# Expert stage of a mixture-of-experts network: 64 slots for each expert in place of 128 for each group, two experts at a time in the column halves of TensorE, fp32 weights used as loaded

## The chip, the core and the metric

One core of a Trainium2 chip runs the whole network in one launch. The metric is the device time of an execution in microseconds (us); the time before is the median of three runs. Engines are named as in the profile: PE is TensorE's matmul, PEld its weight load, DVE VectorE, ACT ScalarE, POOL GpSimd, SP SyncE, whose queue issues the weight loads.

## What is computed

Two blocks with 256 tokens of width 1024. The first has two layers; each has a mixer, a residual and layer norm, and then 16 experts in four groups. The experts are what the change is about:

```python
def hier_moe(x, w_group, b_group, w_router, b_router, w_gate, w_up, w_down):
    ...
    probs_g = jax.nn.softmax((xf @ w_group + b_group).astype(jnp.float32), axis=-1)
    p_top, g_idx = lax.top_k(probs_g, 1)
    logits_e = (xf @ w_router + b_router).astype(jnp.float32).reshape(T, N_GROUPS, EXPERTS_PER_GROUP)
    in_group = jnp.take_along_axis(logits_e, g_idx[:, :, None], axis=1)[:, 0]
    probs_in = jax.nn.softmax(in_group, axis=-1)
    w_top, e_local = lax.top_k(probs_in, TOP_K_IN_GROUP)
    ...
    h = jax.nn.silu(jnp.einsum('td,edf->tef', xf, w_gate)) * jnp.einsum('td,edf->tef', xf, w_up)
    y = jnp.einsum('tef,efd->td', h * gates[:, :, None].astype(h.dtype), w_down)
```

A token goes to one group and to two of its four experts. Each expert has `w_gate` and `w_up` of 1024x256 and `w_down` of 256x1024, fp32: three times 1.05 MB, 50 MB in a layer. The second block (feed-forward parts of width 2816, a latent attention with spatial gating, a short convolution) is not touched.

## The kernel before

Products with large weights are made from two fp32r parts of each operand: `split` and `split_weights` (L130, L177) write the rounded high part on ACT and the rest on DVE, in four pieces of 512 columns, and `mm3` (L118) adds high x high, high x low and low x high.

`moe` (L790) first transposes the mixer's output and multiplies it with the router's weights, normalizes it (`xh`) and splits it (`xs`). `best` (L827) picks the group with five small DVE operations. The token's rank in its group comes from products with a triangular matrix (`pr`, L842), and `pos` is its slot. Then all engines read the largest group count and pass a branch, `tc.If(count > CAP)` (L911), whose body (`every_expert`) handles tokens beyond 128 slots; in the profiled execution it isn't entered. `slots` (L922) makes a 0/1 matrix of two groups, and `gather` (L929) multiplies the tokens with it, so that each group's tokens lie in 128 columns; the result is split again (`xg`, a ring of three groups). The second pair of groups is gathered at step 4.

The loop at L1038 goes over 16 experts. At step n PE does `turned(n-1)` (two transposes of the hidden values, split into `hT`), `up(n)` (L955: 2 x 8 x 3 matmuls of 256 columns into the bank `gu`), and `down(n-1)` (L1016: 2 x 2 x 3 matmuls of 512 columns into the two banks `yd`, which sum over a group's four experts). After each group `scatter` (L1022) splits `yd` and takes it back to token order with eight matmuls into `macc`. `gates` (L858), which needs the second-best expert too, follows the first `up`. `alpha` (L823) adds the residual by fp32 matmuls.

Every expert's load goes into a `raw` tile by SP in program order and waits for a free tile (`weight_tile`, L149); within `moe` there are two more `raw` tiles and one more of each part. In the first layer the projections of the memory for the next mixer (`memory_kv`, `keys` and `values`, L461) are passed in as filler for PE: `keys` ahead of the branch, `values` behind the first gather. Their matmuls stand in the trace partly ahead of where the program has them: the layer that orders the work puts what is ready ahead of what waits. What follows the stage: `after_moe` (L1126), then `stick` (L671), whose first loads are from `w_kv_shared` and `b_w_in`, or `ffn` (L1158).

Two places that are not changed are of use in reading the change: `even_mixer`, lines 1383 to 1393, writes two products into the two halves of the output's partitions (`ps[64 * i:64 * i + 64]`), each with 64 columns of fp32 weights, for four pairs of heads, 256 columns of moving data and then 128; and `alpha` above.

Of the kernel before, what the change touches and what calls it, by code (L numbers as in the profile page):

```python
# [11 lines left out]
F32 = mybir.dt.float32  # L12
F32R = mybir.dt.float32r
# [12 lines left out]
CAP = 128  # L26
SPLITS = 4
MOE_MORE = (2, 1)
LATER = 0
RAW0 = 0  # L30
MOE_SPARE = (6, 0, 2, 99)
# [47 lines left out]
class Net:  # L79
# [57 lines left out]
    @contextmanager  # L137
    def more_buffers(self, raw, parts, turn=0, shift=0):

        names = ("raw", "whi", "wlo")  # L140
        with self.tc.tile_pool(name="more", bufs=1) as p:
            if shift:
                self.shift(p, shift)
            self.extra = [p, dict(zip(names, (raw, parts, parts))), dict.fromkeys(names, 0)]
            self.turn = {"raw": RAW0, "whi": turn, "wlo": turn}
            yield
            self.extra = None

    def weight_tile(self, name, dt):  # L149
        pool, tag, n = self.w, name, 2  # L150
        if self.extra is not None:
            p, more, spare = self.extra
            i = self.turn[name] % (2 + more[name] + spare[name])
            self.turn[name] += 1
            if i >= 2 + more[name]:
                return self.wide_tile(name, dt)
            elif i >= 2:
                pool, n = p, more[name]
# [631 lines left out]
    def moe(self, layer, xh, filler=()):  # L790


        nc, d = self.nc, self.d
        wr, gb, const, gt, bt = self.routed
        with ExitStack() as st:
            p = st.enter_context(self.tc.tile_pool(name="moe", bufs=1))
            st.enter_context(self.more_buffers(*MOE_MORE, turn=2, shift=160))
            early = [self.expert_weights(layer, 0, "w_gate", KD)]
# [39 lines left out]

            gm, go = best(L[:, :, 0:4], "grp")
            gob = p.tile([P, 2, 4], BF, name="grp_b")  # L840
            nc.vector.tensor_copy(gob, go)
            pr = self.aux()  # L842
            self.mm(pr[:, 0:4], self.before, gob[:, 0], True, True)
            self.mm(pr[:, 4:8], self.before, gob[:, 1], True, False)
            self.mm(pr[:, 4:8], self.onesb, gob[:, 0], False, True)
            self.mm(pr[:, 8:12], self.onesb, gob[:, 0], True, False)
            self.mm(pr[:, 8:12], self.onesb, gob[:, 1], False, True)
            most = p.tile([P, 1], F32, name="most")
            nc.vector.tensor_reduce(most, pr[:, 8:12], AX.X, ALU.max)
            mosti = p.tile([P, 1], I32, name="mosti")  # L850
            nc.vector.tensor_copy(mosti, most)
            pos = p.tile([P, 2, 4], F32, name="pos")
            self.ts(pos, go, -4096.0, 4096.0, ALU.mult, ALU.add)
            self.tt(pos, pos, pr[:, 0:8].rearrange("p (a g) -> p a g", a=2), ALU.add)
            rank = p.tile([P, 8], F32, name="rank")
            nc.vector.tensor_copy(rank, pr[:, 0:8])

            def gates():  # L858

                e4 = p.tile([P, 2, 4], F32, name="g_e")  # L860
                self.tt(e4, L[:, :, 0:4], gm[:, :, None].to_broadcast([P, 2, 4]), ALU.subtract)
                self.act(e4, e4, AF.Exp)
                top = p.tile([P, 2], F32, name="p_top")
                nc.vector.tensor_reduce(top, e4, AX.X, ALU.add)
                nc.vector.reciprocal(top, top)
                sel = p.tile([P, 2, 4, 4], F32, name="sel")
                ing = p.tile([P, 2, 4], F32, name="ing")
                for tt in range(2):
                    self.tt(sel[:, tt], L[:, tt, 4:20].rearrange("p (g j) -> p g j", g=4),
                            go[:, tt, :, None].to_broadcast([P, 4, 4]), ALU.mult)  # L870
                    nc.vector.tensor_reduce(ing[:, tt], sel[:, tt].rearrange("p g j -> p j g"), AX.X, ALU.add)
                m1, o1 = best(ing, "one")
                rest = p.tile([P, 2, 4], F32, name="rest")
                self.stt(rest, o1, NEG, ing, ALU.mult, ALU.add)
                m2, o2 = best(rest, "two")
                e2 = p.tile([P, 2], F32, name="e2")
                self.tt(e2, m2, m1, ALU.subtract)
                self.act(e2, e2, AF.Exp)
                w1 = p.tile([P, 2], F32, name="w1")
                self.ts(w1, e2, 1.0, None, ALU.add)  # L880
                nc.vector.reciprocal(w1, w1)
                self.tt(w1, w1, top, ALU.mult)
                self.tt(e2, e2, w1, ALU.mult)
                gj = p.tile([P, 2, 4], F32, name="gj")
                t4 = p.tile([P, 2, 4], F32, name="t4")
                self.tt(gj, o1, w1[:, :, None].to_broadcast([P, 2, 4]), ALU.mult)
                self.tt(t4, o2, e2[:, :, None].to_broadcast([P, 2, 4]), ALU.mult)
                self.tt(gj, gj, t4, ALU.add)
                return gj

            def gates_beyond():

                gj = gates()
                t4 = p.tile([P, 2, 4], F32, name="t4")
                self.ts(t4, rank[:, 0:8].rearrange("p (a g) -> p a g", a=2), float(CAP), None, ALU.is_ge)
                self.tt(t4, t4, go, ALU.mult)
# [10 lines left out]
            for f in filler[:1]:  # L907
                f()
# [604 lines left out]
```

## Time and profile before

| | us |
|---|---|
| median of 3 runs (range) | 1634.55 (1633.69 to 1635.58) |
| the profiled execution's own time | 1639.96 |
| its span, first to last instruction | 1638.2 |
| PE busy, of the span | 1558.1 (95%) |
| DVE busy | 1189.6 (73%) |
| ACT busy | 955.6 (58%) |

Busy time of PE counts a pipelined matmul from its start to its modelled end; the distance between two starts is what a matmul costs in a row of them. In a timeline, a row is "start us, duration us, engine, line, operation, out<-in, shape, count", and several equal instructions in a row are merged; behind it in brackets stands the idle time before it and what ended it. `128*64 128x256` is a weight tile of 128 rows and 64 columns and moving data of 128x256.

### The profile page before, as it was taken

What the parts mean: (1) busy time and instruction counts of PE and PEld (TensorE: products, weight loads), DVE (VectorE), ACT (ScalarE), POOL (GpSimd) and SP (SyncE); (2) the same over time, 40 slices, a digit from 0 to 9 for tenths busy, and PEclk for the clock granted to TensorE, in tenths of its full rate; (3) what the DMA queues carried; (4) which work ended last, traced back from release to release, by engine and by line L of the source; (5) the groups of instructions that cost most, each with busy time, mean ns of one, the idle gap of its engine ahead of it and who ended that gap; (6) DMA issues with size and microseconds to landing.
All of it is one profiled execution on the core that took longest, in us unless ns stands there. A gap on an engine that the chain in (4) does not pass through costs nothing.

```text
span 1638.2 us, 27858 instructions
## 1 busy us (share of the span) xinstructions
PE 1558.1 (95%) x10908; PEld 1431.6 (87%) x10908; DVE 1189.6 (73%) x2448; ACT 955.6 (58%) x1929; POOL 37.6 (2%) x52
## 2 busy tenths in 40 slices
PE   7999879998896999989999999999999999999998
PEld 6998778997775889879988879998899989999986
DVE  6987788987566999896655787665566647766754
ACT  5566677875755887765444656544554445454533
POOL 3000100001000000010000000000000000000000
PEclk9999989999998999999999999999999999999999
DMA  7234547992435589666553547555565547555551
GB/s 230 89 122 155 196 172 275 365 333 88 137 134 198 217 309 346 251 208 206 190 183 99 178 148 226 192 194 180 185 203 186 188 141 233 204 175 193 195 176 60
DMA packets 183710, 317.72 MB, mean 194 GB/s; under 512 B 5755, under 2 KB 135728, under 8 KB 171280
## 3 DMA queue, kind: packets, MB, share of 16 engines
q1 hardware_dynamic: 180976, 309.52, 55.2%
q0 software_dynamic: 2304, 5.78, 1.2%
q8 instruction: 90, 1.47, 0.4%
q14 instruction: 52, 0.43, 0.1%
q10 hardware_dynamic: 288, 0.52, 0.1%
HBM read 314.75 MB, written 1.05 MB: 193 GB/s over the span
## 4 chain that ended last, share of the span: by engine, by line
PE 63%; DVE 2%; ACT 1%; DMA 0%; issue 0%; ACTq 0%
PE acc L116 52%; PE gu L116 5%; PE yd L116 3%; PE aux L116 2%; DVE wlo L105 1%; PE macc L116 1%; PE aux L325 1%; ACT whi L97 1%; DMA raw<-in_w_up_dram 0%; ACT xTh L97 0%; PE gu L1006 0%; PE aux L1374 0%; ACT xgh L97 0%; DVE nt_u L113 0%; DVE ln_st L420 0%
## 5 line engine op out<-in xcount | busy, mean ns | idle before, releaser
L97 ACT ACTIVATE whi<-raw 128x512 fp32r<-128x512 f32 (+3 forms) x1204 | 653.0, 612 | 475.4 <-issue 239.8
L105 DVE TENSOR_TENSOR wlo<-raw,whi 128x512 fp32r<-128x512 f32 (+3 forms) x1204 | 758.5, 677 | 192.2 <-ACT whi L97 190.0
L116 PE MATMUL acc<-xTh,wlo 128*128 128x256 f32 x1824 | 507.4, 278 | 4.3 <-DVE wlo L105 4.3
L116 PE MATMUL acc<-xTh,whi 128*128 128x256 f32 x1824 | 508.3, 279 | 1.2 <-ACT xTh L97 1.2
L116 PE MATMUL acc<-xTl,whi 128*128 128x256 f32 x1824 | 507.7, 279 | 1.2 <-DVE xTl L105 1.1
L116 PEld LDWEIGHTS acc<-xTh,wlo 128*128 128x128 f32 x1824 | 344.4, 189 | 5.6 <-DVE wlo L105 5.1
L116 PEld LDWEIGHTS acc<-xTl,whi 128*128 128x128 f32 x1824 | 344.6, 189 | 2.5 <-DVE xTl L105 1.7
L116 PEld LDWEIGHTS acc<-xTh,whi 128*128 128x128 f32 x1824 | 344.3, 189 | 2.2 <-ACT xTh L97 1.8
L116 PE MATMUL gu<-whi,xgh 128*128 128x256 f32 x512 | 147.8, 289 | 0.0
L116 PE MATMUL gu<-whi,xgl 128*128 128x256 f32 x512 | 144.9, 283 | 2.1 <-DVE xgl L105 2.1
L116 PE MATMUL gu<-wlo,xgh 128*128 128x256 f32 x512 | 145.0, 283 | 0.8 <-DVE wlo L105 0.8
L116 PE MATMUL acc<-whi,hTl 128*128 128x512 f32 x352 | 137.7, 391 | 0.0
L116 PE MATMUL acc<-wlo,hTh 128*128 128x512 f32 x352 | 137.7, 391 | 0.0
L116 PE MATMUL acc<-whi,hTh 128*128 128x512 f32 x352 | 137.7, 391 | 0.0
L116 PEld LDWEIGHTS gu<-whi,xgl 128*128 128x128 f32 x512 | 97.7, 191 | 3.4 <-DVE xgl L105 3.3
L116 PEld LDWEIGHTS gu<-wlo,xgh 128*128 128x128 f32 x512 | 97.6, 191 | 1.7 <-DVE wlo L105 1.2
L116 PEld LDWEIGHTS gu<-whi,xgh 128*128 128x128 f32 x512 | 97.8, 191 | 0.6 <-DVE hTl L105 0.2
L105 DVE TENSOR_TENSOR u<-acc,rms_R 128x512 f32<-128x512 f32 x44 | 30.4, 691 | 84.0 <-PE acc L116 83.8
L116 PEld LDWEIGHTS acc<-whi,hTl 128*128 128x128 f32 x352 | 66.1, 188 | 14.5
L116 PEld LDWEIGHTS acc<-wlo,hTh 128*128 128x128 f32 x352 | 66.1, 188 | 14.4
L116 PEld LDWEIGHTS acc<-whi,hTh 128*128 128x128 f32 x352 | 66.1, 188 | 14.4
L105 DVE TENSOR_TENSOR g<-acc,rms_R 128x512 f32<-128x512 f32 x44 | 30.4, 691 | 40.6 <-PE acc L116 40.6
(428 smaller groups left out, 2146.9 us busy)
## 6 DMA issues: line engine op xcount, KB each, us to landing
raw<-in_w_gate_dram SPq DMA_DIRECT2D x32, 1024.0 KB, 5.1
raw<-in_w_up_dram SPq DMA_DIRECT2D x32, 1024.0 KB, 5.3
raw<-in_w_down_dram SPq DMA_DIRECT2D x32, 1024.0 KB, 5.3
raw<-in_ffn_pre_w_gate_dram SPq DMA_DIRECT2D x22, 1024.0 KB, 5.4
raw<-in_ffn_pre_w_up_dram SPq DMA_DIRECT2D x22, 1024.0 KB, 5.4
raw<-in_ffn_post_w_gate_dram SPq DMA_DIRECT2D x22, 1024.0 KB, 5.2
raw<-in_ffn_post_w_up_dram SPq DMA_DIRECT2D x22, 1024.0 KB, 5.3
raw<-in_ffn_pre_w_down_dram SPq DMA_DIRECT2D x20, 1024.0 KB, 5.0
```

The costliest lines, as they stand in the source:

```text
L97: return self.nc.scalar.activation(out, in_, func, **kw)
L105: return self.nc.vector.tensor_tensor(out, a, b, op=op)
L116: self.last_mm = self.nc.tensor.matmul(out, lhsT, rhs, start=start, stop=stop, skip_group_check=True)
L325: self.nc.tensor.transpose(pv[:, i, tt * P:(tt + 1) * P], src(k + i, tt), self.ident)
```

## The change

- Each expert has 64 slots of its own (`CAP`), so a layer has 16 x 64 slots in place of 4 x 128; `best` is run for both experts ahead of the ranking, and the rank is counted per expert.
- Gathered tokens (`xg`) and hidden values (`hT`) are kept in fp32, unsplit; weights are used from the tile into which they were loaded.
- `up(n)` and `down(n)` handle experts 2n and 2n+1: one writes partitions 0 to 63 of the bank and the other 64 to 127, each with 64 columns of stationary data. The loop has eight pairs. `yd` is no longer summed over a group, and each pair is scattered, one step later (`behind`).
- Loads go into ten tiles in turn (`EXPERT_ROOM`): four new ones and the two each of `raw`, `whi` and `wlo`. The first ten are asked for at the head of `moe`, six more behind each `up`.
- `w_down` is read with rows p and 128 + p on a partition in place of 2p and 2p + 1.
- The branch stands behind `gather(0)`, both `slots` and the gates; `keys` and `values` both stand ahead of `gather(0)`. The second gather is at step 1, `alpha` at steps 5 and 6.
- `every_expert` has other tiles and loads `w_down` separately. `more_buffers` loses options that only `moe` used.

```diff
-CAP = 128
+CAP = 64
-MOE_MORE = (2, 1)
+EXPERT_ROOM = ("more", "more", "more", "more", "raw", "raw", "whi", "wlo", "whi", "wlo")
...
-            early = [self.expert_weights(layer, 0, "w_gate", KD)]
+            self.more = st.enter_context(self.tc.tile_pool(name="more", bufs=1))
+            self.asked = 0
+            wanted = [(name, 2 * n + i) for n in range(8) for name in ("w_gate", "w_up", "w_down") for i in range(2)]
+            loaded = {}
+
+            def fetch(n):
+                for name, ex in wanted[:n]:
+                    loaded[name, ex] = self.expert_weights(layer, ex, name)
+                del wanted[:n]
+
+            fetch(len(EXPERT_ROOM))
...
+            for tt in range(2):
+                self.tt(sel[:, tt], L[:, tt, 4:20].rearrange("p (g j) -> p g j", g=4),
+                        go[:, tt, :, None].to_broadcast([P, 4, 4]), ALU.mult)
+                nc.vector.tensor_reduce(ing[:, tt], sel[:, tt].rearrange("p g j -> p j g"), AX.X, ALU.add)
+            m1, o1 = best(ing, "one")
+            rest = p.tile([P, 2, 4], F32, name="rest")
+            self.stt(rest, o1, NEG, ing, ALU.mult, ALU.add)
+            m2, o2 = best(rest, "two")
+            both = p.tile([P, 2, 4], F32, name="both")
+            self.tt(both, o1, o2, ALU.add)
+            M = p.tile([P, 2, 4, 4], F32, name="members")
+            for tt in range(2):
+                self.tt(M[:, tt], both[:, tt, None, :].to_broadcast([P, 4, 4]),
+                        go[:, tt, :, None].to_broadcast([P, 4, 4]), ALU.mult)
...
+            S = self.wide_tile("S", F32R).rearrange("p (a e c) -> p a e c", a=2, e=16)
+
+            def slots(half):
+                es = slice(8 * half, 8 * half + 8)
                 for tt in range(2):
+                    self.tt(S[:, tt, es], self.slots[:, None, 0:CAP].to_broadcast([P, 8, CAP]),
+                            pos[:, tt, es, None].to_broadcast([P, 8, CAP]), ALU.is_equal)
+
+            xg = [p.tile([P, KD, 8 * CAP], F32, name=f"xg{i}") for i in range(2)]
+
+            def gather(half):
+                Sf = S[:, :, 8 * half:8 * half + 8].rearrange("p a e c -> p a (e c)")
+                for k in range(KD):
+                    pv = self.aux()
+                    for tt in range(2):
+                        for part in range(2):
+                            self.mm(pv, xs[part][:, tt, k], Sf[:, tt], tt + part == 0, tt + part == 2)
+                    g, b = gb[:, 0, k:k + 1], gb[:, 1, k:k + 1]
+                    if k % 2:
+                        self.act(xg[half][:, k], pv, AF.Identity, scale=g, bias=b)
+                    else:
+                        self.ts(xg[half][:, k], pv, g, b, ALU.mult, ALU.add)
+
+            for f in filler:
+                f()
+            slots(0)
+            gather(0)
+            slots(1)
...
             count = nc.values_load(mosti[0:1, 0:1], min_val=0, max_val=T)
             with self.tc.If(count > CAP):
...
+            def up(n):
                 ps = self.aux("gu")
+                for part, name in enumerate(("w_gate", "w_up")):
+                    w = [loaded[name, 2 * n + i].rearrange("p (k f) -> p k f", k=KD) for i in range(2)]
                     for k in range(KD):
+                        for i in range(2):
+                            o = (2 * (n % 4) + i) * CAP
+                            self.mm(ps[64 * i:64 * i + 64, part * 256:(part + 1) * 256],
+                                    xg[n // 4][:, k, o:o + CAP], w[i][:, k], part + k == 0, k == KD - 1)
                 return ps
...
+            def slot_gates():
+                pg = self.aux()[:, 0:8 * 48].rearrange("p (n c e) -> p n c e", n=8, c=3)
+                for n in range(8):
+                    for tt in range(2):
+                        self.mm(pg[:, n], Sb[tt][:, n * P:(n + 1) * P], g3[:, tt], n + tt == 0, tt == 1)
+                for i in range(2):
+                    for n in range(8):
+                        rows = slice(64 * i, 64 * i + 64)
+                        nc.vector.tensor_reduce(gs[rows, n:n + 1], pg[rows, n, :, 2 * n + i], AX.X, ALU.add)
...
+            def turned(n, ps, h):
+
+                for k in range(2):
+                    nc.tensor.transpose(ps[:, k * P:(k + 1) * P], h[:, k * P:(k + 1) * P], self.ident)
                 for tt in range(2):
+                    nc.tensor.transpose(ps[:, (2 + tt) * P:(3 + tt) * P],
+                                        S[:, tt, 2 * n:2 * n + 2].rearrange("p e c -> p (e c)").bitcast(F32), self.ident)
...
+            def down(n, hT, yd):
+                w = [loaded["w_down", 2 * n + i].rearrange("p (k f) -> p k f", k=2) for i in range(2)]
                 for half in range(2):
                     for k in range(2):
+                        for i in range(2):
+                            self.mm(yd[half][64 * i:64 * i + 64], hT[:, k, 64 * i:64 * i + 64],
+                                    w[i][:, k, half * 512:(half + 1) * 512], k == 0, k == 1)
...
+            for n in range(9):
                 if ahead is not None:
+                    m, ps0, h0, done = ahead
+                    hT, ST = turned(m, ps0, h0)
+                if n < 8:
+                    ps = up(n)
+                    if n == 0:
+                        with self.tc.issue_after(parted.ins):
+                            for tt in range(2):
+                                self.act(Sb[tt], S[:, tt].rearrange("p e c -> p (e c)").bitcast(F32), AF.Copy)
+                        slot_gates()
+                    now = (n, ps) + gated(n, ps)
+                    fetch(6)
+                if behind is not None:
+                    scatter(*behind)
+                    behind = None
                 if ahead is not None:
+                    yd = [self.aux("yd") for _ in range(2)]
+                    down(m, hT, yd)
+                    behind = m, ST, parts(yd)
+                if n == 1:
+                    gather(1)
...
+            scatter(*behind)
...
-        return self.weights(self.d[name][layer, ex].rearrange("(p k) f -> p k f", k=k), k, 2048 // k)
...
+        room = EXPERT_ROOM[self.asked % len(EXPERT_ROOM)]
+        self.asked += 1
...
+        if room == "more":
+            to = self.more.tile([P, 2048], F32, name="more", bufs=4)
+        else:
+            size = 2048 if room == "raw" else 2080
+            to = self.w.tile([P, size], F32, name="e" + room, tag=room, bufs=2)[:, 0:2048]
+        self.nc.sync.dma_start(to.rearrange("p (k f) -> p k f", k=src.shape[1]), src)
+        return to
```

## Rows read from the trace of the kernel before

**Rows 1.** The page: busy us, share of the span, and instructions of each engine.
```profile
PE 1558.1 (95%) x10908; PEld 1431.6 (87%) x10908; DVE 1189.6 (73%) x2448; ACT 955.6 (58%) x1929; POOL 37.6 (2%) x52
```

**Rows 2.** Instructions of `gu` and `macc`, each layer: ns min/median/max, first and last start.
```profile
L116 PE MATMUL gu<-whi,xgh x256: 276/281/682, 210.3 to 374.1; 128*128 128x256 f32 x128
L116 PE MATMUL gu<-whi,xgh x256: 276/281/682, 536.4 to 687.2; 128*128 128x256 f32 x128
L116 PE MATMUL macc<-yl,ST x8: 387/396/398, 349.2 to 383.0; 128*128 128x512 f32 x8
L116 PE MATMUL macc<-yl,ST x8: 387/397/475, 662.7 to 696.1; 128*128 128x512 f32 x8
```

**Rows 3.** Windows: length; PE, PEld, DVE, ACT, POOL busy; clock, DMA share, GB/s.
```profile
210.00:383.00 173.00, 160.93 (x1083) 145.97 (x1083) 150.54 (x296) 132.22 (x261) 1.62 (x3) 0.96 0.75 278
536.00:698.00 162.00, 157.04 (x1085) 142.36 (x1083) 148.00 (x284) 127.30 (x254) 0.53 (x1) 1.00 0.77 288
600.00:620.00 20.00, 20.00 (x139) 18.04 (x139) 19.96 (x36) 16.92 (x34) 0.00 (x0) 1.00 1.01 397
```

**Rows 4.** Timeline of PE: neighbours in `down` and in the first `up`.
```profile
300.06 0.39 PE L116 MATMUL yd<-whi,hTl 128*128 128x512 f32 x1
300.29 0.39 PE L116 MATMUL yd<-whi,hTh 128*128 128x512 f32 x1
...
536.36 0.28 PE L116 MATMUL gu<-whi,xgh 128*128 128x256 f32 x1
536.48 0.28 PE L116 MATMUL gu<-wlo,xgh 128*128 128x256 f32 x1
```

**Rows 5.** Groups by line over the span: busy us, mean ns, idle before.
```profile
L105 DVE TENSOR_TENSOR wlo<-raw,whi 128x512 fp32r<-128x512 f32 (+3 forms) x1204 | 758.5, 677 | 192.2 <-ACT whi L97 190.0 <-ACT scx L97 0.4
L97 ACT ACTIVATE whi<-raw 128x512 fp32r<-128x512 f32 (+3 forms) x1204 | 653.0, 612 | 475.4 <-issue 239.8 <-PE acc L116 180.6 <-DMA raw<-in_a_w_in_dram 13.8
L116 PE MATMUL macc<-x,alpha 128*128 128x512 f32 x16 | 7.8, 592 | 0.0
```

**Rows 6.** Timeline of PE: one fp32 product, products in column halves, the one behind.
```profile
273.25 1.02 PE L116 MATMUL macc<-x,alpha 128*128 128x512 f32 x2
...
974.83 2.82 PE L116 MATMUL aux<-pT,vs 128*64 128x256 f32 x32
977.58 0.50 PE L116 MATMUL acc<-whi,mixTh 128*128 128x512 f32 x1
```

**Rows 7.** DMA issues from 492 to 698 us: count, KB each, median us to landing.
```profile
raw<-in_w_gate_dram SPq DMA_DIRECT2D x15, 1024.0 KB, 5.2
```

**Rows 8.** Timeline of SP's queue: first layer's end, second layer's start.
```profile
364.13 0.38 SPq L170 DMA_DIRECT2D raw<-in_w_kv_shared_dram  x1
...
491.62 0.34 SPq L170 DMA_DIRECT2D raw<-in_w_gate_dram  x1
...
517.43 0.33 SPq L170 DMA_DIRECT2D raw<-in_w_up_dram  x1
544.40 0.34 SPq L170 DMA_DIRECT2D raw<-in_w_down_dram  x1
```

**Rows 9.** Window, instructions of `wlo` alone: length; PE, PEld, DVE busy; clock, DMA.
```profile
503.00:517.00 14.00, 4.63 (x12) 2.07 (x11) 7.84 (x13) 1.00 0.58 195
```

**Rows 10.** Timeline of the second layer's routing: selection, and behind the branch.
```profile
521.49 0.16 DVE L830 TENSOR_REDUCE grp_m<-logits 128x2 f32<-128x8 f32 x1
521.68 0.17 DVE L105 TENSOR_TENSOR grp_o<-logits,grp_m 128x8 f32<-128x8 f32 x1
...
529.92 0.87 DVE L109 TENSOR_SCALAR S<-c,pos 128x128 fp32r<-128x128 f32 x4 [4.51 <-DVEq L911]
530.55 0.55 PE L116 MATMUL aux<-S,xsh 128*128 128x256 f32 x1 [5.60 <-DVE S L109]
```

**Rows 11.** Timeline of PE: neighbours in the first gather of the second layer.
```profile
530.90 0.41 PE L116 MATMUL aux<-S,xsl 128*128 128x256 f32 x1
531.11 0.41 PE L116 MATMUL aux<-S,xsh 128*128 128x256 f32 x1
```

**Rows 12.** Windows, all engines: columns as in Rows 3.
```profile
220.00:240.00 20.00, 14.44 (x93) 13.62 (x93) 12.83 (x35) 12.63 (x24) 0.00 (x0) 0.74 0.49 181
500.00:520.00 20.00, 16.97 (x97) 14.41 (x95) 17.76 (x46) 14.77 (x23) 0.00 (x0) 1.00 0.67 231
```

More of the change, by code (lines that the diff above doesn't have):

```diff
@@ L839, in moe @@
             gm, go = best(L[:, :, 0:4], "grp")
[L840 to L847 removed]
+            sel = p.tile([P, 2, 4, 4], F32, name="sel")
@@ L854, in moe @@
[L854 to L867, printed above, removed]
-                for tt in range(2):
[L869 to L889, printed above, removed]
@@ L949, in moe @@
-            Ss = {0: slots(0)}
-            gather(0, Ss[0])
-            early.append(self.expert_weights(layer, 0, "w_up", KD))
-            for f in filler[1:]:
-                f()
-            def up(g, ws):
+                over = p.tile([P, 2, 16], F32, name="over")
+                self.ts(over, pos, float(CAP), None, ALU.is_ge)
+                self.tt(over, over, G, ALU.mult)
+                self.every_expert(p, layer, x, xh, gb, xf, over)
+                nc.scalar.preload_act_table_set("silu_and_others")
@@ L1024, in scatter, with parts @@
+            def parts(yd):
+                out = []
                 for half in range(2):
@@ L1026, in scatter @@
                     yl = p.tile([P, 512], F32R, name="yl", bufs=2)
-                    scattered = self.split(yh, yl, yd[half])
-                    parts.append((yh, yl))
+                    self.scattered = self.split(yh, yl, yd[half])
+                    out.append((yh, yl))
+                return out
+            def scatter(n, ST, y):
                 for half in range(2):
@@ L1031, in scatter @@
                         for i in range(2):
-                            self.mm(acc[tt][half], ST[:, tt * P:(tt + 1) * P], parts[half][i],
-                                    g + i == 0, g + i == 4)
-                return scattered
+                            self.mm(acc[tt][half], ST[:, tt * P:(tt + 1) * P], y[half][i], n + i == 0, n + i == 8)
             acc = [[self.bank("macc") for _ in range(2)] for _ in range(2)]
-            ahead, slot = None, {}
-            for n in range(17):
-                g, e = divmod(n, 4)
-                if n == MOE_SPARE[0]:
-                    self.extra[2].update(raw=MOE_SPARE[1], whi=MOE_SPARE[2], wlo=MOE_SPARE[2])
-                if n == MOE_SPARE[3]:
-                    self.extra[2].update(raw=0, whi=0, wlo=0)
-                if ahead is not None:
-                    g0, e0, ps0, h0, last, done = ahead
-                    hT = turned(ps0, h0)
-                if n < 16:
-                    ps = up(g, self.gate_and_up(layer, n)) if n else first
-                    if e:
-                        now = (g, e, ps) + gated(slot[g][0], e, ps)
-                if ahead is not None:
-                    if e0 == 0:
-                        yd = [self.aux("yd") for _ in range(2)]
-                    down(e0, hT, self.expert_weights(layer, n - 1, "w_down", 2), yd)
-                    if e0 == 3:
-                        scattered = scatter(g0, yd, slot[g0][1])
-                if n < 16 and e == 0:
-                    slot[g] = by_slot(g)
-                    now = (g, e, ps) + gated(slot[g][0], e, ps)
```

213 lines of the change are left out of this document (83 added, 130 removed).

## The prediction, made before the changed kernel ran

> **What bounds the kernel now.** The first view is the page's busy line: PE has 95% of the span, DVE 73%, ACT 58% [rows 1]; the reader should take from it only that no engine is idle on average and that the stage has to be looked at by itself. The change touches only the two expert stages. They run from the first matmul into `gu` (210.3 and 536.4 us) to the last scatter (383.0 and 696.1 us, 0.4 us long) [rows 2]: 173 and 160 us. The windows over them show PE busy for 161 and 157 us at a granted clock of 0.96 and 1.00, DVE for 151 and 148 us, and DMA at 0.75 to 0.77 of its time [rows 3]. So four resources lie close together, and what the change is worth depends on the second one, not on PE's saving alone.
>
> One expert now costs PE 48 matmuls of 256 columns that start 0.12 us apart, 12 of 512 columns 0.23 us apart, two transposes and a quarter of eight scatter matmuls [rows 4]: 48 x 0.12 + 12 x 0.23 + 0.24 + 0.46 = 9.2 us. The splits cost DVE 12 x 0.68 = 8.1 us, ACT 12 x 0.61 = 7.3 us per expert [rows 5]. Its three loads of 1.049 MB take 3 x 2.64 = 7.9 us at the 397 GB/s that the window 600 to 620 holds with DMA at 1.01 [rows 3]. PE binds, DVE and DMA are 12 to 14% behind. 16 x 9.2 = 147 us of each stage is this; the other 13 to 26 us are the second gather, the `alpha` products and waits.
>
> **Part 1: PE's work per pair of experts.** The new matmuls take fp32 operands. The row of `macc<-x,alpha` counts 16 instructions for the 8 products in the code, so one fp32 product is two passes [rows 5]; the two passes of one 512-column product take 1.02 us together with 0.59 us for the second, so one pass starts 0.43 us after the other [rows 5, 6]. That is 0.84 ns a column and pass: 0.43 us for an fp32 product of 256 columns, 0.86 us for 512. Two products into the two halves of the columns: lines 1383 to 1393 make 8 of 256 and 8 of 128 columns this way, 32 instructions in 2.82 us with the tail of the last [rows 6]. In a row they would take 8 x 0.43 + 8 x 0.215 = 5.2 us; without the tail of about 0.27 us it is half of that. The halves do run beside each other. A pair of experts then costs PE: gate and up 16 steps x 0.43 = 6.9 us, down 4 x 0.86 = 3.4, four transposes at most 0.5, eight scatter matmuls 8 x 0.23 = 1.8: 12.6 us, against 18.4 now.
>
> The Trainium skill speaks against this in "TensorEngine Tiling (Array Packing)", section Key Properties: a change of tiling mode drains the engine. The trace shows such a change as a duration of 0.50 us for the first full matmul behind the halves [rows 6], against 0.39 us [rows 4]; at four changes a pair by that price it would be 0.4 us, which lies in waits that the next part finds.
>
> **Part 2: loads.** A pair needs six loads: 6 x 2.64 = 15.9 us, above PE's 12.6. So the stage goes over from PE to the loads. They are issued by SP in order, into ten buffers, the first ten ahead of the router, and each later one waits until its buffer's last reader is done. A load of its own takes 5.2 us from issue to landing [rows 7]. The ten are asked for at about 491 us (the first load now goes at 491.6 [rows 8]) and need some 30 us; the first product comes at about 540 us, so they are there. SP now issues nothing between 517.4 and 544.4 us in this stretch [rows 8]; that pause stays, since all ten buffers are full.
>
> In the steady part two things compete. By bandwidth a pair takes 15.9 us. By the ring: the up weights of pair n+2 go into the buffers that down(n) frees, and down(n) stands behind up(n+1) on PE: half of up 3.4 + scatter 1.8 + down 3.4 + 5.2 to landing + 2.6 for the second = 16.4 us. I take 16.5.
>
> **Part 3: splits removed.** All 48 x 4 splits per stage on ACT and DVE go: 192 x 0.68 = 130 us of DVE and 192 x 0.61 = 117 us of ACT [rows 5], hidden behind PE today. Worth nothing in the steady part. In the routing stretch they stand between the small operations on DVE: 7.8 us of `wlo` between 503 and 517 us [rows 9]. I take 4 us of gain in the second layer and 2 in the first, where part of them belongs to the memory projection and stays. Ends: 0 and 7.8.
>
> **Part 4: routing and gather.** Eighteen small DVE operations move ahead of the ranking (selection of two experts, membership): they start 0.2 us apart [rows 10], 3.6 us on the path. Slots: two operations of 128x512 at 0.68 us [rows 5] ahead of the gather in place of two or four of 0.2 to 0.3: +0.5. gather(0) has 32 matmuls of 512 columns where 256 stood: at the full clock 32 x 0.23 = 7.4 us, at the clock that PE has after its idle time 0.21 us per 256 columns [rows 11], so 13.7; I take 10.5, the middle. Now 32 of them take 5.8 us (530.55 to 536.36) [rows 10, 4]: +4.7 us in the second layer; in the first, twenty `values()` matmuls that now stand among them move ahead, so +1.7. The branch moves behind the gather: PE's 5.6 us and DVE's 4.5 us of idle time there [rows 10] are paid once in either place. Bounds: 0, if the gather's evictions cover it, to +5 if PE is cold once more behind it. The POOL issues that wait at the branch feed only the stage's end. First product: 536.4 + 3.6 + 0.5 + 4.7 - 4 = 541 us; first layer 210.3 + 3.6 + 0.5 + 1.7 - 2 = 214 us.
>
> The branch is not taken: routing the inputs by the reference gives at most 40 tokens for an expert in the first layer and 44 in the second, under 64.
>
> **Part 5: the stage from its first product.** up(0) 6.9 us, 3 more for the low clock; loads restart when the gate half is used, at 6 us. up(2)'s weights are there 5.2 + 5 x 2.64 later, at 24 us, if down(0) is early; if PE does slot gates, up(1) and down(0) strictly in order and waits some 3.5 us for the sixteen small reductions before the first transposes, down(0) ends at 25 and they land at 33. Five more pairs at 16.5: 107 or 116. Behind the last up weights: 3.4 + scatter 1.8 + down(6) 3.4 + 0.5 + scatter 1.8 + down(7) 3.4 + eviction of two halves 2.2 + scatter 1.8 = 18 us. 125 or 134; I take 129, and 3 us for dips of the clock (below): 132. gather(1), 7.4 us, the `alpha` products, 3.4, and slot gates lie in the 4 us that PE waits in each pair. ACT and DVE lose more than they gain.
>
> What follows: kv_shared went at 364.1 us, 19 us ahead of the end [rows 8]; behind the change it waits in SP's queue for a buffer that up(7) frees, some 15 us ahead of the end, and 5.2 us suffice. Cost nothing; without that cover up to 5 us.
>
> **Sum.** First layer: 214 + 132 = 346 against 383.4: -37. Second: 541 + 132 = 673 against 696.5: -23.5. The profiled execution took 1639.96 us (span 1638.2); less 60.5 it is 1579.5. The median of the runs lies 5.4 us lower, so 1574 us.
>
> **Rivals.** (a) PE's clock falls in every pair, because PE now waits for loads. For it: between 220 and 240 us, where PE was busy 14.4 of 20 us with waits between, the granted clock averaged 0.74, so 2.4 GHz and 1.2 GHz by turns; 12.6 of 16.5 us is not far from that. Against it: 17.0 of 20 us kept 1.00 between 500 and 520 [rows 12]. The waits here would be two of 2 to 3 us per pair. At 0.74 PE's pair is 17 us and the ring 8.6 / 0.74 + 7.8 = 19.4, three more than I took, over seven pairs and a longer tail about 25 us per layer: 60 - 50, 1624 us. The Trainium skill states it as a rule in "TensorE: Matmul & The Clock Gate", section HAM oscillation: short bursts with load waits between them go back to half clock each time. By that rule the trace's 0.74 is the case to expect; 1.00 at 17 of 20 us is where the trace does not bear it out.
>
> (b) Slower than before: the halves don't overlap in this form, since here both halves read fresh weights at every step where the case of rows 6 did so for 16 products. Then gate and up take 13.8 us, down 6.9, a pair 23; PE binds, 8 x 23 + 7.4 + 3.4 + 18 = 213 us from the first product: +44 and +58 against now, 1634 + 102 = 1736. It decides from a pair time of about 18 us on. Rows 6 are against it. A milder form on the same side is (a) with the clock at 1.2 GHz through the stage, 25 us per pair, but a PE that is busy without a pause got 1.00 in this trace.
>
> (c) The ring does not bind and the loads come at full rate: no splits, down early, first product as early as now. 120 us from 212 and 537: -51 and -39, 1544 us. For it: work that is ready was put ahead in this kernel (the `values()` matmuls among the gather's). Against: it needs every one of these.
>
> (d) The change doesn't do what it says: an expert overflows and the fallback runs, 48 more loads a layer at 5.2 us, 250 us each. Only other inputs would do that.
>
> **Chances.** Forecast 0.62; (a) 0.18; (c) 0.10; (b) and its milder form 0.08; (d) and others 0.02. Bounds: the unknown prices of parts 3 to 5 move a layer by -12 to +14 us, two layers 1550 to 1602; (c) adds 1544 below, and half of (a) up to 1612 above. Range 1542 to 1612. A measurement of this kernel tells 0.2%, about 3 us, from no change. Faster than that: forecast, (c) and nearly all of (a): 0.87; within: 0.04, the far end of (a); slower: 0.09.
>
> **What would show it.** Right: no `whi` or `wlo` split of expert weights; `gu` products of 128*64 in pairs, a pair of experts every 16 to 17 us, DMA above 0.9 in that stretch, PE near three quarters busy and waiting for DMA; first `gu` near 214 and, in the second layer, near 541 - 37 = 504. Wrong: PE without a pause in the stage (b), a granted clock under 0.85 there (a), a first product later than 225 us, or a pair well under 16 us.

## The result and the profile after

| | before | changed | ratio (95% interval) |
|---|---|---|---|
| median of the runs beside each other, us | 1635.07 | 1565.5 | 0.9564 (0.9536 to 0.9592) |
| profiled execution, span, us | 1638.2 | 1562.8 | |

The forecast was 1574, from a profiled execution 5 us above its median. By the spans the change is worth 75.4 us against 60.5 forecast; by the medians, which leave those 5 us out, it is 69.6. The timelines of both kernels (first matmul into `gu`, end of the last scatter) split it:

| us | before | forecast | changed | forecast missed by |
|---|---|---|---|---|
| to the first product, layer 1 | 210.3 | 214 | 215.9 | +1.9 |
| stage, layer 1 | 173.1 | 132 | 121.7 | -10.3 |
| to the first product, layer 2 | 152.9 | 157.6 | 156.5 | -1.1 |
| stage, layer 2 | 160.1 | 132 | 121.7 | -10.3 |
| the rest of the span | 941.7 | 941.7 | 947.0 | +5.3 |

The page's busy line of the changed kernel, to set beside [rows 1]: DVE has lost 235 us and ACT 220, while the splits counted on the page fall from 1204 to 820 on each; PE has lost 67.

```profile
PE 1490.8 (95%) x10332; PEld 1293.2 (83%) x10332; DVE 954.9 (61%) x2024; ACT 735.2 (47%) x1481; POOL 37.7 (2%) x52
```

Its windows over both stages and 20 us in the first (columns as in [rows 3]): PE is busy without a pause in the 20 us, at a granted clock of 1.00 (2.4 GHz), and DMA is busy all the time beside it.

```profile
216.00:338.00 122.00, 120.10 (x792) 72.00 (x792) 28.44 (x58) 22.02 (x40) 1.61 (x3) 1.00 0.88 349
494.00:616.00 122.00, 120.20 (x792) 72.14 (x792) 28.19 (x58) 21.76 (x39) 0.53 (x1) 1.00 0.89 353
296.00:316.00 20.00, 20.00 (x133) 12.11 (x131) 3.20 (x6) 2.37 (x6) 0.00 (x0) 1.00 1.02 415
```

Its timeline of PE: the first gate and up, and one whole pair, from one pair of transposes to the next.

```profile
215.91 7.13 PE L114 MATMUL gu<-more,xg 128*64 128x256 f32 x64 [3.14 <-DVEq L942]
...
252.15 3.65 PE L114 MATMUL yd<-more,hT 128*64 128x512 f32 x16
255.73 0.44 PE L991 MATMUL gu<-ident,h 128*128 128x128 f32 x2
256.00 0.38 PE L993 MATMUL gu<-ident,S 128*128 128x128 f32 x2
256.32 0.43 PE L114 MATMUL gu<-ewhi,xg 128*64 128x256 f32 x1
256.32 0.43 PE L114 MATMUL gu<-ewlo,xg 128*64 128x256 f32 x1
...
259.82 3.62 PE L114 MATMUL gu<-more,xg 128*64 128x256 f32 x32
263.37 0.50 PE L114 MATMUL macc<-yh,ST 128*128 128x512 f32 x1
...
265.43 0.64 PE L114 MATMUL yd<-ewhi,hT 128*64 128x512 f32 x1
...
269.02 0.44 PE L991 MATMUL gu<-ident,h 128*128 128x128 f32 x2
```

`ewhi` and `ewlo` start at the same time: the halves overlap. The pair takes 13.29 us: transposes 0.59 (255.73 to 256.32), gate and up 7.05, scatter 2.06, down 3.59. Of the seven distances between transposes in the stage only this one and the one before it are plain pairs; all seven are 16.3 (with the second gather), 13.2, 13.3, 15.6, 17.3, 12.9 and 15.6 us, 14.9 in the mean.

### The profile page after: what moved, and what is told of

Read it like the earlier page. It is cut to its first block, busy times and chain, and to the rows that moved or that the text cites. A ratio compares the mean times of both kernels' runs of the same rounds, so it can differ in the third digit from the quotient of the medians.

```text
span 1562.8 us, 25664 instructions
## 1 busy us (share of the span) xinstructions
PE 1490.8 (95%) x10332; PEld 1293.2 (83%) x10332; DVE 954.9 (61%) x2024; ACT 735.2 (47%) x1481; POOL 37.7 (2%) x52
## 4 chain that ended last, share of the span: by engine, by line
PE 64%; DVE 2%; DMA 1%; ACT 0%; issue 0%; SPq 0%; ACTq 0%; DVEq 0%
PE acc L114 55%; PE gu L114 4%; PE aux L114 2%; PE yd L114 2%; PE macc L114 1%; DVE wlo L103 1%; DMA raw<-in_ffn_pre_w_up_dram 1%; PE aux L319 1%; DMA raw<-in_ffn_post_w_gate_dram 0%; DVE x L103 0%; PE aux L1371 0%; ACT whi L95 0%; ACT rms_sq L95 0%; DVE nt_u L111 0%; DVE qT L1330 0%
## 5 line engine op out<-in xcount | busy, mean ns | idle before, releaser
L95 ACT ACTIVATE whi<-raw 128x512 fp32r<-128x512 f32 (+4 forms) x820 | 440.2, 604 | 449.8 <-issue 240.0
L103 DVE TENSOR_TENSOR wlo<-raw,whi 128x512 fp32r<-128x512 f32 (+4 forms) x820 | 517.3, 672 | 178.8 <-ACT whi L95 177.6
L103 DVE TENSOR_TENSOR yl<-yd,yh 128x512 fp32r<-128x512 f32 x32 | 22.1, 690 | 79.8 <-ACT yh L95 79.6
L114 PE MATMUL gu<-more,xg 128*64 128x256 f32 x448 | 56.7, 382 | 4.7 <-DVEq L942 3.1
L95 ACT ACTIVATE yh<-yd 128x512 fp32r<-128x512 f32 x32 | 19.1, 598 | 84.0 <-PE yd L114 83.5
L114 PE MATMUL acc<-wlo,xTh 128*128 128x384 f32 (+2 forms) x160 | 55.8, 348 | 0.0
L114 PE MATMUL acc<-whi,xTl 128*128 128x384 f32 (+2 forms) x160 | 55.7, 349 | 0.0
L114 PEld LDWEIGHTS gu<-more,xg 128*64 128x64 f32 x448 | 36.5, 137 | 23.2 <-issue 9.7
L114 PE MATMUL acc<-whi,xTh 128*128 128x384 f32 (+2 forms) x160 | 55.5, 349 | 0.1
```

Source lines behind the costliest of these rows:

```text
L95: return self.nc.scalar.activation(out, in_, func, **kw)
L103: return self.nc.vector.tensor_tensor(out, a, b, op=op)
L114: self.last_mm = self.nc.tensor.matmul(out, lhsT, rhs, start=start, stop=stop, skip_group_check=True)
```

## Experiments

A kernel's ratio is to runs of the kernel before on the same chip; the changed kernel's is 0.9564 in this measure. "Stage" is from the first product to the end of the last scatter.

**In turn.** Both halves' products are the same, in another order (in `down` likewise):

```diff
-                    for k in range(KD):
-                        for i in range(2):
+                    for i in range(2):
+                        for k in range(KD):
```

> In up and down, all products of one expert's half of the columns are issued first, then those of the other half; every product stays as it is. Theory (the two halves run beside each other only while neighbouring instructions alternate between them): the first gate-and-up block takes about 13.8 us in place of 7.1, down about 6.9 in place of 3.6, a pair costs PE about 23 us and PE alone binds; each expert stage takes some 195 to 205 us from its first product in place of 122, the whole some 150 to 165 us more, about 1720 us. Rival 1 (the halves overlap whatever the order, since the engine has a queue for each): no change, 1565 us. Rival 2 (the order of the products is put right on the way to the engine, by a layer that puts ready work ahead): no change either, with gu rows in which the halves still alternate.

Measured: 1635.55 us, ratio 0.9987 (0.9968 to 1.0005); stages 160.2 and 158.6 us. Neither theory's number. Timeline of PE:

```profile
215.64 13.24 PE L114 MATMUL gu<-more,xg 128*64 128x256 f32 x64 [3.32 <-DVEq L942]
...
266.91 3.71 PE L114 MATMUL yd<-more,hT 128*64 128x512 f32 x16
...
271.14 3.02 PE L114 MATMUL gu<-ewhi,xg 128*64 128x256 f32 x13
273.78 0.43 PE L114 MATMUL gu<-ewlo,xg 128*64 128x256 f32 x1
273.99 0.38 PE L114 MATMUL gu<-ewhi,xg 128*64 128x256 f32 x1
274.05 0.38 PE L114 MATMUL gu<-ewlo,xg 128*64 128x256 f32 x1
```

Each half's eight products (16 passes) run alone until the last three or so, and only then does the other half start beside them (273.78). In `down` one half's run is two products, four passes, and all of it takes 3.71 us against 3.65 in the changed kernel: hardly a loss. So the mechanism of the theory holds, and its size was off: the other half starts once no more than three instructions of the running half stand between the two, in `down` from the first one on (266.91 and 266.93). Gate and up take 11.5 us a pair (253.32 to 264.86), not 13.8, and the pair 17.8 (the two without other work), not 23; the first gate and up, 13.24 us, lie at a granted clock of 0.87. The order of two loops is worth the whole gain of the change.

**Which resource binds the changed stage.** Three kernels: `w_down` loaded once a layer (the two `raw` tiles hold it to the last `down`, and the other eight places serve gate and up); half the scatter; both.

```diff
-            wanted = [(name, 2 * n + i) for n in range(8) for name in ("w_gate", "w_up", "w_down") for i in range(2)]
+            wanted = [(name, 2 * n + i) for n in range(8) for name in ("w_gate", "w_up", "w_down") for i in range(2)
+                      if n == 0 or name != "w_down"]
```
```diff
-                        for i in range(2):
-                            self.mm(acc[tt][half], ST[:, tt * P:(tt + 1) * P], y[half][i], n + i == 0, n + i == 8)
+                        self.mm(acc[tt][half], ST[:, tt * P:(tt + 1) * P], y[half][0], n == 0, n == 7)
```

> Leaves out 14 of the 48 weight loads of each layer: w_down of the first pair serves all eight pairs. PE's work is the same; four tiles fewer in the ring. In the changed kernel's stages PE is busy 120.1 of 122.0 us and the DMA rate is 415 GB/s, so both lie at their limit. Theory A (the loads bind, PE's busy time contains waits that its modelled ends hide): the stage from its first product shrinks from 122 to PE's own sum of about 113 us, 7 to 9 us a layer, together 1547 to 1552 us. Theory B (PE binds by itself, the loads keep pace): within 2 us of 1565. In both, the 12.6 us of PE per pair shows as the distance between the first gu products of two neighbouring pairs if loads do not bind.

> Leaves out the low part of the scatter: four matmuls of 512 columns a pair in place of eight, 0.92 us of PE less for each of eight pairs, 7.4 us a layer; the loads are untouched. Theory A (the loads bind): only the last scatter is shorter, 1 us a layer, 1563 us. Theory B (PE binds): 7 us a layer, about 1551 us.

> Leaves out both the 14 w_down loads and the low part of the scatter of each layer. Each alone shortened the stage from its first product (121.7 us) little: without the loads 120.2, without the scatter's low part (7.4 us of PE) 117.9. Without the loads the distance from one pair's transposes to the next's is 13.3 us, PE without a pause. Theory (PE binds, and the loads stand just behind it): with both gone PE alone is left, 120.2 less 7.4 = 113 us a stage, about 1536 us. Rival (a chain through ACT and DVE, h, hT and the parts of yd, is the second limit, not the loads): 117 us or more, as without the scatter's low part alone, 1543 us or more.

| | median, us | ratio (interval) | stages, us | from the first transposes, us |
|---|---|---|---|---|
| changed kernel | 1565.5 | 0.9564 (0.9536 to 0.9592) | 121.7, 121.7 | 111.4, 111.4 |
| fewer loads | 1550.46 | 0.9475 (0.9443 to 0.9507) | 120.4, 120.0 | 108.4, 108.4 |
| half the scatter | 1555.33 | 0.9502 (0.9472 to 0.9532) | 118.0, 117.8 | 106.0, 107.1 |
| both | 1537.8 | 0.9384 (0.936 to 0.9407) | 112.5, 113.7 | 100.5, 100.5 |

The last column leaves out the first gate and up, because the clock was low in it in most of these stages. With fewer loads it took 8.75 us in the first layer, in place of 7.06, at a granted clock of 0.80 and so in part at 1.2 GHz; the window over it (columns as in [rows 3]):

```profile
214.30:223.00 8.70, 8.66 (x64) 6.46 (x64) 0.00 (x0) 0.00 (x0) 0.00 (x0) 0.80 0.26 89
```

Counted so, a stage loses 3.0 us without 14 of 48 loads, 4.3 to 5.4 without 7.4 us of PE, and 10.9 without both: the 7.4, the 3.0 and half a us more. PE binds. The 3.0 us are not waits for loads. In the changed kernel and the four others with the same expert stage (no branch, the splits behind, and the two on top, all below) the last column is 111.4 in all ten stages, to 0.03 us, and PE waits for no load in it; nor does it with half the scatter. What differs is the order of PE's instructions. The pairs without the loads keep the program's order, 13.29 us of PE:

```profile
255.85 0.44 PE L992 MATMUL gu<-ident,h 128*128 128x128 f32 x2
...
269.14 0.44 PE L992 MATMUL gu<-ident,h 128*128 128x128 f32 x2
...
282.43 0.44 PE L992 MATMUL gu<-ident,h 128*128 128x128 f32 x2
```

In the changed kernel gate and up, scatter and down are mixed from the fourth pair on, so that one half partly runs with nothing beside it (269.60), and the last pair's `h` comes late:

```profile
269.60 0.65 PE L114 MATMUL gu<-eraw,xg 128*64 128x256 f32 x2
270.18 0.50 PE L114 MATMUL macc<-yh,ST 128*128 128x512 f32 x1
...
272.24 0.64 PE L114 MATMUL yd<-more,hT 128*64 128x512 f32 x1
272.25 0.65 PE L114 MATMUL gu<-eraw,xg 128*64 128x256 f32 x2
...
330.50 0.44 PE L991 MATMUL gu<-ident,h 128*128 128x128 f32 x2 [0.99 <-DVE h L111]
```

From the transposes at 269 us to the stage's end it takes 68.6 us, without the loads 65.6; about 1 us of the difference is waiting for `h` and `hT`, the rest PE's own. Why the order came out so, no run shows. The loads need at most the 118 us of the stage with half the scatter.

The median of the first kernel fell by 15 us, as its theory A had it, but for another reason: 9 us of it lie between the stages (156.5 became 147.5). The `raw` tiles come free late there, so the next stage's first load goes out 2.8 us ahead of the stage's end, in place of 8.5, its splits come behind the normalization (the first on DVE at 339.19 us), and PE's waits for `y` and `sph`, 6.27 and 5.09 us in the changed kernel, are shorter:

```profile
331.94 0.38 SPq L164 DMA_DIRECT2D raw<-in_w_kv_shared_dram  x1
```
```profile
338.45 3.51 PE L319 MATMUL aux<-ident,y 128*128 128x128 f32 x16 [3.76 <-ACT y L95]
...
358.34 0.38 PE L114 MATMUL aux<-sph,c 128*128 128x256 f32 x1 [0.95 <-ACT sph L95]
```

That led to the kernels on the time given back, below.

**A ring of eight.**

```diff
-EXPERT_ROOM = ("more", "more", "more", "more", "raw", "raw", "whi", "wlo", "whi", "wlo")
+EXPERT_ROOM = ("more", "more", "raw", "raw", "whi", "wlo", "whi", "wlo")
```

> The ring of weight tiles has eight places in place of ten, so a load of the steady part waits for a reader that stands later. My predicted step (the ring binds: the up weights of pair n+2 wait for the buffers that down(n) frees): with eight places every load hangs on a reader some third of a pair nearer, the DMA share in the stage falls clearly below 1, and each stage gets 10 to 25 us longer, 1585 to 1615 us. Rival (the ring does not bind, loads come at the full rate and PE is about as fast): under 4 us a layer, at most 1573 us.

Measured: 1581.94 us, ratio 0.9654 (0.9617 to 0.969); stages 131.4 and 134.4 us, 10 and 13 more; the total lies just under the 1585 expected. With eight places the ring binds; with ten it does not. Its windows show what that brings:

```profile
256.00:276.00 20.00, 15.44 (x90) 9.36 (x90) 1.68 (x4) 1.62 (x4) 0.00 (x0) 0.83 0.78 313
276.00:296.00 20.00, 18.10 (x102) 11.10 (x100) 2.72 (x5) 2.31 (x5) 0.00 (x0) 0.91 0.93 370
```

PE waits for loads (4.6 us at 261 us, 1.9 at 279), and in the same stretches the granted clock goes between its two levels, 0.83 and 0.91 on average. This is rival (a) in small. The rule in the Trainium skill, "TensorE: Matmul & The Clock Gate", section HAM oscillation (load waits between short bursts cost the clock too), agrees with these two rows; the changed kernel at 1.00 has no such waits.

**What bound the stage before.** In the kernel before, each layer's first split parts of each weight name serve all experts; loads and PE's work stay.

```diff
-        return self.weights(self.d[name][layer, ex].rearrange("(p k) f -> p k f", k=k), k, 2048 // k)
+        if (layer, name) not in self.once:
+            self.once[layer, name] = self.weights(...)
+        else:
+            raw = self.weight_tile("raw", F32)
...
+            self.act(self.touch, raw[:, 0:1], AF.Copy)
+        return self.once[layer, name]
```

> The kernel before, with each layer's expert weights split only once for each of the three names and the two parts then used for all 16 experts; all loads are still made, and ACT reads one column of each. Leaves out the other 15/16 of the splits; PE's work and the bytes are the same. Theory (PE bound the stage before, at 9.2 us an expert): the stages of 173 and 160 us fall at most to 147 us plus the 10 to 13 us outside the experts, so 13 and 0 to 5 us, and with what the routing stretch loses of splits 10 to 25 us in all: 1610 to 1625 us. Rival (the splits on ACT and DVE bound it, and the gain of the change comes from their removal): the larger part of the gain of 70 us, 1590 us or less.

Measured: 1626.32 us, ratio 0.9935 (0.9912 to 0.9957); stages 162.4 and 158.7 us, 10.8 and 1.5 less than before. That is just above the 1610 to 1625 expected and far from the rival's 1590: taking the splits alone away is worth 0.65%. PE bound the second stage. How much of the 10.8 us in the first were splits, and how much the clock (0.96 before, 0.99 here), is not separated.

**The branch.** The changed kernel without `tc.If(count > CAP)` and its body.

> The changed kernel without the branch and its body (the fallback for more than 64 tokens an expert), which is not entered with these inputs. Theory (PE's idle time behind the first gather is on the path, as the first product waits for the branch that all engines pass): the first product comes 3 to 4 us earlier in each layer, and the stage keeps its length, 6 to 8 us in all, about 1558 us. Rival (the loads bind, and since the ring is full until the first product and restarts with it, the gain is the same): 1558 as well. Other rival (the work that now fills the wait, the gates and slots, only moves behind it): within 3 us of 1565.

Measured: 1556.35 us, ratio 0.9506 (0.9482 to 0.9531), stages 121.7 us. In the first layer the first product comes at 210.8 us; in the changed kernel and the eight others made from it with its order of loops it came between 213.8 and 217.6. In the second layer only 0.6 us of the stretch between the stages goes, not 3 to 4, and 2.3 us go behind it. The theory holds for the first layer alone; the last 2.3 us are not explained (944.7 us, where half the scatter, the ring of eight and the turned places, all with the same code there, have 945.1 to 947.0).

**The time given back: tiles or order.** The ring's places in another order (first), and the next stage's first splits behind the normalization (second).

```diff
+EXPERT_ROOM = ("raw", "raw", "whi", "wlo", "more", "more", "more", "more", "whi", "wlo")
```
```diff
-                    self.ts(y[:, tt, cs], acc[tt][half], rs, nm, ALU.mult, ALU.add)
+                    lastd = self.ts(y[:, tt, cs], acc[tt][half], rs, nm, ALU.mult, ALU.add)
...
-                    self.act(y[:, tt, cs], acc[tt][half], AF.Identity, scale=rs, bias=nm)
+                    lasta = self.act(y[:, tt, cs], acc[tt][half], AF.Identity, scale=rs, bias=nm)
+        self.first_behind = lastd, lasta
```

> The ring's places in another order, so that in the last pairs the two raw tiles and one of each part come free earlier, those in which the next stage's first weights are loaded and split. The lead of the changed kernel falls from 80.6 us at the second stage's end to 76.3 behind the next stage's start. Theory (the next stage's loads and splits come late, since their tiles are held by the last pairs): 1 to 3 us a layer less, 1560 us. Rival (the splits wait in the engines' order among the small normalization operations, whatever the tiles): no change.

> The changed kernel; the next stage's first splits are placed behind the normalization's last operations on ACT and DVE in place of among them. In the changed kernel four low-part subtractions of 0.64 to 0.68 us stand among the small normalization operations at 339 to 342 us and PE then waits 6.3 us for the normalized tokens, where it waited 4.4 us in the kernel before. Theory (the splits delay the normalization): about 2 us a layer less, 1561 us. Rival (the splits are then late by as much for PE's next products): no change, or 1 to 2 us more.

Measured: 1565.68 us, ratio 0.957 (0.9546 to 0.9594), no change, though the next stage's first load went out at 318.75 us in place of 329.12; and 1558.9 us, 0.9525 (0.9499 to 0.9551). The order counts, not the tiles. Timeline of PE behind the first stage of the changed kernel, idle time in brackets:

```profile
343.88 3.68 PE L319 MATMUL aux<-ident,y 128*128 128x128 f32 x16 [6.27 <-ACT y L95]
...
357.58 0.39 PE L114 MATMUL acc<-xTh,wlo 128*128 128x256 f32 x1 [1.25 <-DVE wlo L103]
...
370.14 0.58 PE L114 MATMUL aux<-sph,c 128*128 128x256 f32 x1 [5.09 <-ACT sph L95]
```

With the splits behind:

```profile
343.58 3.81 PE L319 MATMUL aux<-ident,y 128*128 128x128 f32 x16 [4.24 <-ACT y L95]
...
364.59 0.38 PE L114 MATMUL aux<-sph,c 128*128 128x256 f32 x1 [1.46 <-ACT sph L95]
...
638.86 0.77 PE L114 MATMUL aux<-ident,rms_rs 128*128 128x128 f32 x2 [5.30 <-DVE rms_rs L111]
```

More went than the 2 us expected: between the stages 156.5 became 147.0. The wait of 5.09 us shrank too. In the changed kernel ACT has a split ahead of `sph` in its order, and that split waits for a load:

```profile
369.15 0.63 ACT L95 ACTIVATE whi<-raw 128x512 fp32r<-128x512 f32 x1 [4.02 <-DMA raw<-in_b_w_in_dram]
369.69 0.71 ACT L95 ACTIVATE sph<-sb_s 128x256 fp32r<-128x256 f32 x2
```

That load goes out at 360.35 us, behind two loads of POOL's queue (`ln_g`, `ln_b`, 359.71 and 360.27), and lands 8.7 us later; with the splits behind it goes at 356.97, ahead of those two, and lands after 4.9. The kernel before has this wait too, so it is not time that the change gave back; of the wait for `y` (4.38 us there) some 2 us are.

```profile
414.73 0.58 PE L116 MATMUL aux<-sph,c 128*128 128x256 f32 x1 [5.93 <-ACT sph L97]
```

Behind the second stage the kernel with the splits behind lost 1.8 us (the wait at 638.86).

**Two versions on top.** Splits behind in the first layer only; and splits behind in both, with the addition of the bias to `x` on DVE behind the second stage.

```diff
-            nc.gpsimd.tensor_tensor(x[:, tt], x[:, tt], bt, op=ALU.add)
+            if gain is None:
+                nc.gpsimd.tensor_tensor(x[:, tt], x[:, tt], bt, op=ALU.add)
+            else:
+                self.tt(x[:, tt], x[:, tt], bt, ALU.add)
```

> The changed kernel with the next stage's first splits behind the normalization in the first layer only. Theory (the gain of that move comes from the first layer, where it also lets the next loads go out earlier, and it costs 1.9 us in the second): 1556 to 1558 us. Rival (the two layers differ by chance of the clock's dips): 1560 us or more.

> The changed kernel with the next stage's first splits behind the normalization, and behind the second expert stage the addition of the bias to x on DVE in place of POOL. With the splits moved alone the time between the stages fell from 156.5 to 147.0 us, but the part behind the second stage took 1.9 us more: PE waited 5.30 us at 633.6 us for rms_rs, which waits for the two additions on POOL, 9.31 us from 623.4 us. Theory (these additions are on the path): on DVE they take some 2.4 us, rms_rs comes about 5 us earlier, and the kernel is 4 to 6 us faster than with the splits moved alone, 1553 to 1555 us. Rival (the next weights' splits on DVE are then later by as much, and PE waits for them instead): within 2 us of 1559 us.

Measured: first layer only 1557.11 us, 0.951 (0.9497 to 0.9523); with `x` on DVE 1551.22 us, 0.9474 (0.9457 to 0.949). The second beats the changed kernel by 0.9%, the intervals apart. Between the stages it takes 146.9 us and behind the second 940.2, 6.8 less than the changed kernel and 1.5 less than the kernel before: what had been given back is regained. The move of `x` without that of the splits was not run. The additions in it, on DVE:

```profile
622.10 2.36 DVE L103 TENSOR_TENSOR x<-x,ln_b 128x1024 f32<-128x1024 f32 x2
```

## Why the prediction was right, and where a step failed

The total was right; the limit was not. The forecast had the loads bind through the ring, with PE busy three quarters of the time. PE bound, and two of the forecast's own signs of being wrong came: PE without a pause, and pairs well under 16 us. That the total still came near has some luck in it: the stages gave 20.6 us more than forecast, and the rest took 6 of them back.

- PE's pair: 12.6 us forecast, 13.29 measured. The products were right (gate and up 6.9 against 7.05, down 3.4 against 3.59); the difference of 0.7 us lies in blocks that are each 0.14 to 0.2 us longer than their products, so the four changes between halves and full width cost nearer 0.7 us a pair than the 0.4 estimated.
- The loads' pair: 15.9 us at 397 GB/s; they reached 415, so 6 x 1.049 MB take 15.2. That is still above 13.29, but ten of 48 loads lie ahead of the stage, and PE has the second gather and `alpha` to do: over the stage the loads need at most 118 us (half the scatter), PE in its order 121.7. I took the longer pair time for the bound of the whole stage and did not count the start that the ten tiles give.
- The ring, 16.5 us a pair: **this step failed**, and it is the miss of 10 us in each stage. I let the up weights of pair n+2 wait for the buffers of down(n), as if the places came round strictly in turn. In the changed kernel's timeline of SP the up weights of the fourth pair go out at 246.73 us:

```profile
219.58 0.90 SPq L1078 DMA_DIRECT2D more<-in_w_down_dram  x2
...
246.73 0.80 SPq L1078 DMA_DIRECT2D more<-in_w_up_dram  x2
...
314.58 0.46 SPq L1078 DMA_DIRECT2D ewlo<-in_w_down_dram  x1
329.12 0.37 SPq L164 DMA_DIRECT2D raw<-in_w_kv_shared_dram  x1
```

  That is when the third pair's gate, which reads `more` too, ends on PE (243.03 + 3.67), and 9 us before the down products from `more` end (252.15 + 3.65). So among the four `more` tiles a load took those that came free first. The five pairs that I priced by the ring, 82.5 us together, took 72.4 (242.50 to 314.88), with PE as their limit. A ring of eight shows what a binding ring does: 131 to 134 us. That this is near my 132 is chance, since I had priced ten places.
- Splits: worth nothing in the steady part, as forecast: the second stage lost 1.5 us with the splits made once.
- Routing and gather: second layer +4.6 us forecast, +3.6 measured; first layer 1.9 us later than forecast.
- Three us for dips of the clock and 3 for the first `up`: not paid; clock 1.00 from 216 us on.
- The next stage's late loads: "nothing, without cover up to 5". The first load went out 8.5 us ahead of the first stage's end, not 15, in time for PE, but its splits fell among the small operations of the normalization. Behind the second stage 5.3 us were lost, some 4 of them where PE waits for `rms_rs`, behind the additions on POOL (3.4 us, against 1.2 before), and then runs in part at the lower clock (0.91 from 637.9 to 656 us, 1.00 in the kernel before). Moving the splits alone made that stretch longer still (948.8 us); with `x` on DVE as well the loss was gone (940.2).
- Rivals: (a) did not come, since PE never waits for long; (b) needs the other order of loops; (c) gave 120 us for the stage, and that is what came, but its earlier first products did not. The forecast's total came out 15 us short in the spans: 20.6 too little from the stages, 6 too much elsewhere.

## What to carry to other kernels

When work moves into halves of the array's columns, alternate the halves from one instruction to the next, or in runs of two: in runs of eight the whole gain was lost here. When two resources come within a few per cent, compare their sums over the stage, with what lies loaded ahead of it, not their times per step, and look up which buffer a load really takes before giving a ring a price. After a stage gets shorter, look at what stands among the small operations behind it: there 14 us were to be had, a fifth of the change's own gain, though not all of it was the change's doing. And a PE that is busy without a pause can still lose time to the order of its instructions, some 2 us a stage here.

## What was not expected of the hardware

DVE and POOL hold each other up. Undisturbed, a subtraction of a split takes 0.68 us on DVE and an addition of the bias 2.44 us on POOL. In the changed kernel two additions on POOL stand beside the first two of four subtractions on DVE, which take 2.9 us each:

```profile
634.84 6.08 POOL L1151 TENSOR_TENSOR x<-x,ln_b 128x1024 f32<-128x1024 f32 x2 [103.47 <-PE acc L114]
```
```profile
635.75 6.92 DVE L103 TENSOR_TENSOR wlo<-raw,whi 128x512 fp32r<-128x512 f32 x4
```

With the splits behind, DVE keeps its speed (six in 3.69 us), and it is POOL that waits: the first addition takes 6.91 us, the second, when DVE is done, 2.44.

```profile
624.31 3.69 DVE L103 TENSOR_TENSOR wlo<-raw,whi 128x512 fp32r<-128x512 f32 x6
```
```profile
623.40 9.31 POOL L1152 TENSOR_TENSOR x<-x,ln_b 128x1024 f32<-128x1024 f32 x2 [99.86 <-PE acc L114]
```

In both kernels an operation of DVE is under way when POOL begins, so these rows do not show what decides which of the two waits.

The Trainium skill, "Trainium Architecture — The Big Picture", section What this means for kernel authors, has the two share a pair of ports under an exclusive lock, not a split of the bandwidth. The rows agree with it: each time one side waits for whole instructions of the other. The two additions on DVE instead cost 2.36 us.
